# A list scheduler's figures and its model of transfers, replaced in a two-layer decoder kernel

## The chip, the cores and the metric

The kernel runs on one core of one Trainium2 chip. The metric is the device time of one execution in microseconds (us), lower is better. Traces come from the hardware profiler; in them PE is TensorE (matmuls), PEld its weight loads, DVE is VectorE, ACT is ScalarE, POOL is GpSimd and SP is SyncE, whose queue issues most DMAs.

## The reference

Two layers, post-norm. Layer 0 mixes tokens by a chunked causal gMLP, layer 1 by causal attention in one block of 256 keys (12 heads of 64); beside each runs a 4-head cross-attention into 256 memory tokens. Sequence 256, width 1024, feed-forward width 2816, float32 throughout.

```python
for i in range(2):
    if i == 0:
        u, v, q_mem = split(x @ a_w_in)          # 768, 768, 256
        mix = gmlp_mixer(u, v, ...)              # gelu, layer norm of v, W_s v + b, times u
    else:
        q, k, v, q_mem = split(x @ b_w_in)       # 768, 768, 768, 256
        mix = causal_attention(q, k, v)          # 12 heads
    mem_out = memory_cross_attention(q_mem, mem, w_mem_kv[i])
    sub = concatenate([mix, mem_out]) @ w_mix_out[i]
    x = layer_norm(ALPHA * x + sub)
    g, u = split(x @ w_ffn_in[i])                # 2 x 2816
    x = layer_norm(ALPHA * x + (silu(g) * u) @ w_ffn_out[i])
return x
```

## The kernel before

**Work.** Every weight is read once, as float32, in units of mostly 1 MiB (128 x 2048) that SP's queue loads from one flat array in the order in which they are used. A unit lands in a raw buffer (a ring of four, `raw`; two of the four quarter matrices of an S unit, below, go to buffers of their own, tags `gb` and `vbig`). Each half of it is then split in two: ACT copies it to a rounded `hi` (a CAST in the trace), DVE subtracts to get `lo` (a TENSOR_TENSOR into the same tile, `spl_...`). PE multiplies in three passes: hi by hi, hi by lo, lo by hi. Ten split halves can be held at a time (`HALF_BUFS`). The feed-forward goes by chunks of 256 columns: an R step takes one chunk directly (tiles `pf`, `pg`), an S unit takes two chunks together in seven products M1, M5, M2, M3, M6, M7, M4 (a Strassen form; tiles `X`, `Y`, `Z`, with letter f for layer 0 and g for layer 1). Three of the products need sums of quarter matrices, which DVE adds (`raw_s<-raw_s,raw_s`); the sum for M7 is made by a DMA from POOL's queue that adds into the raw buffer while it lands. After M6, ACT copies the sum from `X` to `u2`; M7 adds into `X` again, and so has to wait for that copy. Each layer has four S units. The kernel interleaves the products with the second matrix of the feed-forward (`fof`, `fog`).

**Order.** The code doesn't call the engines. It records operations (`Plan.add`, `Op`), and `Plan.emit` issues them in an order that `Plan.order` has worked out at build time by simulating the program with a duration for every operation. In every engine's queue the instructions run in that order, and one that waits holds up those behind it. PE's own order is that in which the code records its operations; the planner moves DVE, ACT, POOL and SP, and chooses buffer slots.

- `Op.cost` gives an operation `hold` (time before the engine takes the next) and `lat` (time until its result is there).
- `deadlines` puts PE's operations end to end and works back from them to a latest time `late` for every other operation, with `delay` as the distance of two dependent ones.
- `simulate` takes at each step the operation that can start first on any engine, the one with the smallest `late` among equals, and looks ahead: when one with an earlier `late` will become ready while the candidate runs, it takes a shorter one in between, or lets the engine idle. The three numbers of a setting (`slip`, `idle`, `margin`) rule that. `lost` sums the time that PE idles in the simulation.
- `order` runs the five settings of `TRIALS` and keeps the order with the least `lost`.
- A transfer in `simulate` before the change: one link of 437 bytes a ns for all queues, 2.3 us from issue to its first byte, 2.1 times the bytes and at least 7.8 us for a DMA of POOL.

Of the kernel before, what the change touches and what calls it, by code (L numbers as in the profile page):

```python
# [209 lines left out]
class Op:  # L210
# [13 lines left out]
    def cost(self):  # L224

        w = max([v.width() for v in self.writes + self.reads] or [1])
        e, n = self.engine, self.name
        if n == "dma_start":
            v = (self.writes or self.reads)[0]
            self.bytes = 4 * v.ap.ap[0][1] * v.width()  # L230
            self.hold, self.lat = (900 if e == "gpsimd" else 400), 0
        elif e == "tensor":
            w = self.args[2].width() if n == "matmul" else P
            f32 = n == "matmul" and self.args[2].root.dtype == F32
            self.hold = max(104, (w + 32) / 2.4) if not f32 else 0.85 * w
            self.lat = 200 + 0.37 * w if not f32 else self.hold + 270
        elif e == "vector":
            slow = n in ("tensor_scalar_mul", "tensor_scalar_add") or n == "tensor_copy"
            self.lat = 225 + 0.48 * w if n == "tensor_scalar_mul" and w > 8 else 150 + 1.042 * w
            self.hold = self.lat - 82  # L240
        elif e == "scalar":
            self.lat = 190 + 0.842 * w + (200 if "accum_out" in self.kw else 0)
            self.hold = self.lat - 100
        else:
            self.lat = self.hold = 700 + 2.5 * w if w < 8 else 250 + 2.0 * w


class Plan:
# [48 lines left out]
    def delay(self, a, b):  # L297

        if a.engine == b.engine and a.name != "dma_start":
            return a.hold  # L300
        if a.name == "dma_start":
            return 2300 + a.bytes / 400 if a.engine != "gpsimd" else 2300 + a.bytes / 180
        return a.lat + (50 if b.engine == "tensor" else 33)

    def deadlines(self):
        t = 4300
        for op in self.ops:
            if op.engine == "tensor":
                op.late = t
                t += op.hold  # L310
        for op in self.ops:
            for o in op.before.values():
                o.after.append(op)
        slots, last, follow = {}, {}, {}
        for op in self.ops:
            for b in op.roots:
                last[b] = op.n
        for op in self.ops:
            for b in op.roots:
                if b.tile is None and b.slot is None:  # L320
                    free = slots.setdefault(b.tag, [(0, i, None) for i in range(b.bufs)])
                    free.sort()
                    n, b.slot, was = free.pop(0)
                    if was:
# [12 lines left out]

    def order(self):
        self.deadlines()
        best = None  # L340
        for trial in self.TRIALS:
            for op in self.ops:
                for b in op.roots:
                    b.slot, b.last, b.left = None, 0.0, 0
            for op in self.ops:
                for b in op.roots:
                    b.left += 1
            out, lost = self.simulate(*trial)
            self.trials.append(lost)
            if best is None or lost < best[0]:  # L350
                best = lost, [(op, op.opens, op.call, op.start, op.end, [b.slot for b in op.opens]) for op in out]
        for op, op.opens, op.call, op.start, op.end, slots in best[1]:
            for b, b.slot in zip(op.opens, slots):
                pass
        return [x[0] for x in best[1]]

    def simulate(self, slip, idle, margin):
# [2 lines left out]
        head = {e: 0 for e in by_late}  # L360
        gone = set()
        free = {e: 0.0 for e in self.ENGINES}
        busy = dict(free)
        waiting = {op.n: len(op.before) for op in self.ops}
        at = {op.n: 0.0 for op in self.ops}
# [2 lines left out]
        for op in self.ops:  # L368
            for b in op.roots:
                if b.tile is None:  # L370
                    t = tags.setdefault(b.tag, {"queue": [], "slots": [(0.0, i) for i in range(b.bufs)]})
                    if b not in t["queue"]:
                        t["queue"].append(b)
        pe = [op for op in self.ops if op.engine == "tensor"]
        ip = 0
        link = 0.0
        for op in self.ops:
            if not waiting[op.n]:
                for e in op.calls():
                    ready[e].append(op)  # L380
        out = []

        def opening(op):

            t0 = at[op.n]
            for b in op.roots:
                if b.slot is not None or b.tile is not None:
                    continue
# [5 lines left out]
                fit = [x for x in t["slots"] if not b.whole or x[1] in whole]  # L394
                if not fit:
                    return None
                t0 = max(t0, min(fit)[0])
            return t0

        def hope(op, memo, depth):  # L400

            if op in memo:
                return memo[op]
            t = at[op.n]
            if waiting[op.n]:
                for o in op.before.values():
                    if o in gone:
# [12 lines left out]
        while len(out) < len(self.ops):  # L420
# [64 lines left out]
            for b in op.opens:  # L485
                q = tags[b.tag]
                q["queue"].remove(b)
                fit = [x for x in q["slots"] if x[0] <= t] if not b.whole else [x for x in q["slots"] if x[1] in whole]
                s = min([x for x in fit if x[1] not in whole] or fit) if b.psum else min(q["slots"])
                q["slots"].remove(s)  # L490
                b.slot = s[1]
            if e == "tensor" and (op.name == "transpose" or op.kw["start"]):
# [2 lines left out]
                if b.tag == "mm":  # L495
                    (whole.add if full else whole.discard)(b.slot)
            if op.name == "dma_start":
                size = op.bytes * (2.1 if e == "gpsimd" else 1) / 437
                link = max(link, t + 2300) + size
                end = max(link, t + 7800 if e == "gpsimd" else 0) + 100  # L500
            else:
                end = t + op.call.lat
            op.end = end
            out.append(op)
            for o in op.after:
                w = t + op.call.hold if o.engine == e and not o.other and op.name != "dma_start" else end + (50 if o.engine == "tensor" else 33)
                at[o.n] = max(at[o.n], w)
                waiting[o.n] -= 1
                if not waiting[o.n] and o.engine != "tensor":
                    for e2 in o.calls():  # L510
                        ready[e2].append(o)
            for b in op.roots:
                b.left -= 1
                b.last = max(b.last, end + 33)
                if not b.left and b.slot is not None:
                    tags[b.tag]["slots"].append((b.last, b.slot))
        return out, lost

    def emit(self):
# [934 lines left out]
```

## Time and profile before

| | us |
|---|---|
| median of 3 runs (lowest, highest) | 569.29 (568.52, 570.24) |
| the profiled execution's own time | 569.77 |
| its span, first to last instruction | 568.1 |
| around the span | 1.67 |
| mean granted TensorE clock in the span | 0.997 |

Rows of the trace below come from the profiled execution; "own time" means its 569.77 us. All recorded operations carry one source line, L527, that of the call in `emit`, so groups are told apart by the names of the tiles.

### The profile page before, as it was taken

Reading aid. Unit: us, or ns where it says so; the run is one execution under the profiler, and the core shown is the slowest. Engines: PE = TensorE matmul, PEld = TensorE weight load, DVE = VectorE, ACT = ScalarE, POOL = GpSimd, SP = SyncE. Lnnn points to the kernel's source line nnn. Section 1 sums busy time; section 2 is a strip of 40 time slices with the busy share of each in tenths; the row PEclk is TensorE's granted clock in tenths of the full one; section 3 lists DMA queues with packets and bytes.
Section 4 is the critical chain, followed back from the end, with each engine's and each line's share of the span. In section 5 each row is a group of like instructions: output and inputs, shape, how many; then the busy total and the mean of one; then the engine's idle time right before and its main releaser. Section 6 shows DMA issues by size and latency. Waiting matters only on the chain.

```text
span 568.1 us, 8078 instructions
## 1 busy us (share of the span) xinstructions
PE 554.7 (98%) x3052; PEld 478.0 (84%) x3052; DVE 498.8 (88%) x667; ACT 363.6 (64%) x550; POOL 23.0 (4%) x32
## 2 busy tenths in 40 slices
PE   8999999999999999999999999999999999999994
PEld 7999879887888778888899999888788888878884
DVE  5689889999999999994887889589998999989965
ACT  6676757677676757763446988654766676757710
POOL 2101001000000000000000000000000000000001
PEclk9999999999999999999999999999999999999998
DMA  8999744736856685775367343346448757675502
GB/s 292 359 388 345 308 170 137 291 74 247 228 195 228 195 313 150 295 279 193 118 230 300 141 149 106 118 148 240 149 133 303 213 211 216 212 281 133 207 1 75
DMA packets 21624, 118.89 MB, mean 209 GB/s; under 512 B 2384, under 2 KB 6096, under 8 KB 9168
## 3 DMA queue, kind: packets, MB, share of 16 engines
q1 hardware_dynamic: 20000, 109.45, 52.4%
q0 software_dynamic: 1152, 8.39, 8.0%
q10 hardware_dynamic: 432, 0.52, 0.3%
q8 instruction: 24, 0.39, 0.3%
q14 instruction: 16, 0.13, 0.1%
HBM read 117.31 MB, written 1.05 MB: 208 GB/s over the span
## 4 chain that ended last, share of the span: by engine, by line
PE 47%; DVE 25%; issue 5%; DMA 4%; ACT 3%; DVEq 0%; ACTq 0%
PE fog L527 7%; PE fof L527 7%; DVE spl_s_M L527 6%; PE Xg L527 5%; PE Xf L527 4%; DMA raw_s<-in_w 4%; DVE raw_s L527 4%; PE opc L527 4%; PE bv L527 3%; PE qk L527 3%; PE pg L527 2%; PE Zf L527 2%; PE pf L527 2%; PE Zg L527 2%; DVE spl_w L527 1%
## 5 line engine op out<-in xcount | busy, mean ns | idle before, releaser
L527 ACT CAST spl_s_M<-raw_s 128x1024 fp32r<-128x1024 f32 x112 | 115.4, 1052 | 56.2 <-DVE raw_s L527 20.3
L527 DVE TENSOR_TENSOR spl_s_M<-raw_s,spl_s_M 128x1024 fp32r<-128x1024 f32 x112 | 132.2, 1219 | 5.8 <-ACT spl_s_M L527 5.4
L527 PE MATMUL fog<-spl_w,htg 128*128 128x512 f32 (+1 forms) x282 | 63.7, 378 | 0.0
L527 PE MATMUL fof<-spl_w,htf 128*128 128x512 f32 x264 | 63.7, 392 | 0.0
L527 PEld LDWEIGHTS fog<-spl_w,htg 128*128 128x128 f32 x282 | 50.2, 188 | 9.4
L527 PEld LDWEIGHTS fof<-spl_w,htf 128*128 128x128 f32 x264 | 49.0, 188 | 9.9
L527 DVE TENSOR_TENSOR spl_w<-raw_w,spl_w 128x1024 fp32r<-128x1024 f32 x44 | 53.2, 1218 | 2.3 <-ACT spl_w L527 2.3
L527 DVE TENSOR_TENSOR raw_s<-raw_s,raw_s 128x2048 f32<-128x2048 f32 x24 | 54.9, 2286 | 0.1
L527 ACT CAST spl_w<-raw_w 128x1024 fp32r<-128x1024 f32 x44 | 45.8, 1050 | 13.7 <-PE fog L527 3.8
L527 PE MATMUL qk<-x2T,spl_qk 128*128 128x256 f32 x288 | 36.5, 284 | 0.1
L527 PEld LDWEIGHTS qk<-x2T,spl_qk 128*128 128x128 f32 x288 | 35.2, 192 | 0.4 <-DVE mix L527 0.3
L527 PE MATMUL Xf<-spl_s_M,SfM 128*128 128x512 f32 x96 | 23.2, 390 | 0.6 <-ACT u2f L527 0.6
L527 PE MATMUL Xg<-spl_s_M,SgM 128*128 128x512 f32 x96 | 23.2, 390 | 0.3 <-ACT u2g L527 0.3
L527 PE MATMUL opc<-spl_o,mix 128*128 128x512 f32 x96 | 23.1, 394 | 0.0
L527 PE MATMUL Zf<-spl_s_M,SfM 128*128 128x512 f32 x96 | 23.1, 389 | 0.0
L527 PE MATMUL Zg<-spl_s_M,SgM 128*128 128x512 f32 x96 | 23.1, 389 | 0.0
L527 PE MATMUL Xg<-spl_s_M,x3T 128*128 128x512 f32 x96 | 22.8, 391 | 0.0
L527 PE MATMUL Xf<-spl_s_M,x1T 128*128 128x512 f32 x96 | 22.7, 391 | 0.0
L527 PE MATMUL opa<-spl_o,mix 128*128 128x512 f32 x96 | 22.5, 392 | 0.0
L527 PEld LDWEIGHTS Xf<-spl_s_M,SfM 128*128 128x128 f32 x96 | 17.9, 188 | 4.7 <-ACT u2f L527 1.0
L527 PEld LDWEIGHTS Xg<-spl_s_M,SgM 128*128 128x128 f32 x96 | 17.9, 188 | 4.4 <-ACT u2g L527 0.7
L527 PEld LDWEIGHTS Xg<-spl_s_M,x3T 128*128 128x128 f32 x96 | 17.9, 188 | 4.2 <-DVE m5g L527 0.4
(232 smaller groups left out, 1082.9 us busy)
## 6 DMA issues: line engine op xcount, KB each, us to landing
raw_s<-in_w SPq DMA_DIRECT2D x32, 1024.0 KB, 5.9
raw_w<-in_w SPq DMA_DIRECT2D x22, 1024.0 KB, 5.5
raw_o<-in_w SPq DMA_DIRECT2D x8, 1024.0 KB, 6.4
raw_s<-in_w POOLq DMA_DIRECT2D x8, 1024.0 KB, 8.8
raw_r_A<-in_w SPq DMA_DIRECT2D x6, 1024.0 KB, 4.9
raw_r_B<-in_w SPq DMA_DIRECT2D x6, 1024.0 KB, 4.8
raw_qk<-in_w SPq DMA_DIRECT2D x6, 1024.0 KB, 5.8
raw_u<-in_w SPq DMA_DIRECT2D x3, 1024.0 KB, 9.8
```

What stands on the lines that cost most here:

```text
L527: getattr(getattr(self.nc, c.engine), c.name)(*map(real, c.args), **{k: real(v) for k, v in c.kw.items()})
```

## The change

The figures in `Op.cost` and `delay` are replaced, and the model of transfers becomes a class of its own, `Wire`. It keeps two queues, one for SP and ACT (`hard`) and one for POOL (`soft`), each moving one transfer at a time, at 250, 370 or 428 bytes a ns by the time since the start for the one, 223 for the other, and 155 and 123 when both move. A transfer starts 2.35 us after its issue. It has an `end`, and a later `sure`: 0.2 us after its last byte in the first 20 us, then 1.2 us after it (1.8 us for POOL). Operations that need the data, and buffers that it wrote, count from `sure`. SP may issue its next DMA only when the one eight places before has ended. An operation on DVE or ACT that depends on one of the same engine counts from that one's result plus 35 ns, where it counted from its `hold`; a consumer on POOL counts 500 ns after the result. SP starts at 0.8 us. Nothing else of the kernel is edited: the recorded operations, PE's order and `TRIALS` are the same.

```diff
@@ Op.cost
+        psum = any(v.root.psum for v in self.writes + self.reads)
...
-            self.hold, self.lat = (900 if e == "gpsimd" else 400), 0
+            self.hold, self.lat = (1000 if e == "gpsimd" else 450), 0
...
-            self.lat = 200 + 0.37 * w if not f32 else self.hold + 270
+            self.lat = (205 + 0.36 * w if n == "matmul" else 273) if not f32 else self.hold + 280
         elif e == "vector":
-            slow = n in ("tensor_scalar_mul", "tensor_scalar_add") or n == "tensor_copy"
-            self.lat = 225 + 0.48 * w if n == "tensor_scalar_mul" and w > 8 else 150 + 1.042 * w
+            fast = n == "tensor_scalar_mul" and w > 8
+            self.lat = 225 + 0.48 * w if fast else 152 + 1.042 * w
+            if n == "scalar_tensor_tensor" and not psum:
+                self.lat += 57
             self.hold = self.lat - 82
         elif e == "scalar":
-            self.lat = 190 + 0.842 * w + (200 if "accum_out" in self.kw else 0)
-            self.hold = self.lat - 100
+            self.lat = 190 + 0.842 * w + (90 if "accum_out" in self.kw else 0) - (35 if psum else 0)
+            self.hold = self.lat - 98 + (100 if "accum_out" in self.kw else 0)
         else:
-            self.lat = self.hold = 700 + 2.5 * w if w < 8 else 250 + 2.0 * w
+            self.lat = self.hold = 985 if w < 8 else 300 + 1.4 * w
+
+class Wire:
+
+    HARD, SOFT, BOTH, LANES = ((7000, 250), (30000, 370), (1e12, 428)), 223, (155, 123), 8
+    SPARE = 1200, 1800
+
+    def __init__(self):
+        self.now, self.hard, self.soft, self.sent = 0.0, [], [], []
+
+    def lane(self):
+        return self.sent[-self.LANES].end + 30 if len(self.sent) >= self.LANES else 0.0
+
+    def issue(self, op, t):
+        self.run(t, [self.hard, self.soft])
+        if op.engine == "sync":
+            self.sent.append(op)
+        (self.soft if op.engine == "gpsimd" else self.hard).append([op, t + 2350, op.bytes])
+        self.run(1e12, [[list(x) for x in q] for q in (self.hard, self.soft)])
+
+    def run(self, until, queues):
+        hard, soft = queues
+        now = self.now
+        while (hard or soft) and now < until:
+            live = [bool(q) and q[0][1] <= now for q in queues]
+            edge, hard_rate = next(x for x in self.HARD if now < x[0])
+            rates = self.BOTH if all(live) else (hard_rate * live[0], self.SOFT * live[1])
+            ends = [now + q[0][2] / r for q, r, a in zip(queues, rates, live) if a]
+            stop = min(ends + [edge] + [q[0][1] for q, a in zip(queues, live) if q and not a] + [until])
+            for q, r, a in zip(queues, rates, live):
+                if a:
+                    q[0][2] -= (stop - now) * r
+                    if q[0][2] < 1:
+                        op = q.pop(0)[0]
+                        op.end = stop + 100
+                        op.sure = stop + (self.SPARE[op.engine == "gpsimd"] if stop > 20000 else 200)
+            now = stop
+        if until < 1e12:
+            self.now = until

@@ Plan.delay
-            return a.hold
+            return a.hold if a.engine == "tensor" else a.lat + 35
...
-        return a.lat + (50 if b.engine == "tensor" else 33)
+        return a.lat + {"tensor": 56, "gpsimd": 500}.get(b.engine, 35)

@@ Plan.simulate
+        free["sync"] = 800.0
...
+        def free_at(x):
+            b = x[0]
+            return max([b.last] + [o.sure for o in b.moves]) if b else 0.0
+
         def opening(op):
-            t0 = at[op.n]
+            t0 = max([at[op.n]] + [o.sure for o in op.moves])
+            if op.engine == "sync":
+                t0 = max(t0, wire.lane())
...
-                t0 = max(t0, min(fit)[0])
+                t0 = max(t0, min(map(free_at, fit)))
...
         def hope(op, memo, depth):
-            t = at[op.n]
+            t = max([at[op.n]] + [o.sure for o in op.moves if o in gone])
...
             if op.name == "dma_start":
-                size = op.bytes * (2.1 if e == "gpsimd" else 1) / 437
-                link = max(link, t + 2300) + size
-                end = max(link, t + 7800 if e == "gpsimd" else 0) + 100
+                wire.issue(op, t)
+                end = 0
...
             for o in op.after:
-                w = t + op.call.hold if o.engine == e and not o.other and op.name != "dma_start" else end + (50 if o.engine == "tensor" else 33)
-                at[o.n] = max(at[o.n], w)
+                if op.name != "dma_start":
+                    same = o.engine == e == "tensor"
+                    at[o.n] = max(at[o.n], t + op.call.hold if same else end + {"tensor": 56, "gpsimd": 500}.get(o.engine, 35))
```

## Rows read from the trace of the kernel before

**Rows 1.** Part 1 of the profile's page: busy us of each engine, its share of the span, number of instructions.

```profile
PE 554.7 (98%) x3052; PEld 478.0 (84%) x3052; DVE 498.8 (88%) x667; ACT 363.6 (64%) x550; POOL 23.0 (4%) x32
```

**Rows 2.** The table of stretches: from and to in us, length, then busy us of each engine (and instructions), granted clock, DMA's busy share, GB/s.

```profile
0.00:14.20 14.20, 12.21 (x74) 10.74 (x75) 7.63 (x15) 8.71 (x16) 3.63 (x12) 1.00 0.86 292
14.20:28.40 14.20, 14.20 (x97) 14.20 (x96) 8.52 (x13) 8.81 (x13) 1.64 (x1) 1.00 1.05 359
...
190.00:205.00 15.00, 14.63 (x68) 12.26 (x69) 15.00 (x14) 10.28 (x12) 0.00 (x0) 1.00 0.65 238
...
550.00:568.10 18.10, 10.65 (x64) 9.33 (x62) 11.01 (x25) 0.51 (x1) 2.20 (x3) 0.91 0.18 60
```

**Rows 3.** PE's waits in the whole span: who waited for whom, us in total, times, longest.

```profile
PE sm L527 <- DVE klm L527: 0.6, 1, 0.6
PE Xf L527 <- ACT u2f L527: 0.6, 1, 0.6
PE pu L527 <- DVE spl_u L527: 0.5, 1, 0.5
...
PE tpf L527 <- DVE hf L527: 0.4, 1, 0.4
PE tpf L527 <- DVE m5f L527: 0.4, 1, 0.4
...
PE pf L527 <- DVE x1T L527: 0.3, 1, 0.3
PE Xg L527 <- ACT u2g L527: 0.3, 1, 0.3
PE tpg L527 <- DVE hg L527: 0.2, 1, 0.2
```

**Rows 4.** ACT's waits for landings of weights, same columns.

```profile
ACT spl_s_M L527 <- DMA raw_s<-in_w: 13.6, 5, 4.1
...
ACT spl_o L527 <- DMA raw_o<-in_w: 5.2, 3, 4.3
...
ACT spl_u L527 <- DMA raw_u<-in_w: 4.7, 3, 3.3
```

**Rows 5.** Timelines of ACT and PE around the scores of the memory attention, in layer 0 and (last two rows) layer 1: start us, us, engine, operation, how many in a run, and in brackets the idle time before it and who ended it.

```profile
56.19 1.05 ACT L527 CAST spl_o<-raw_o 128x1024 fp32r<-128x1024 f32 x1 [4.29 <-DMA raw_o<-in_w]
57.15 1.13 ACT L527 CAST kkm<-hkm 64x256 fp32r<-64x256 f32 x3
...
47.16 5.92 PE L527 MATMUL hkm<-memT,spl_km 128*128 128x256 f32 x48
...
58.77 0.28 PE L527 MATMUL sm<-kkm,qqm 128*128 128x256 f32 x1
...
62.80 1.47 PE L527 MATMUL pvm<-spl_vm,memT 128*128 128x256 f32 x11
...
337.37 0.39 PE L527 MATMUL sm<-kkm,qqm 128*128 128x256 f32 x1
...
338.31 0.28 PE L527 MATMUL sm<-klm,qqm 128*128 128x256 f32 x1
```

**Rows 6.** DMA issues: how many, KB of one, median us from issue to landing.

```profile
raw_s<-in_w SPq DMA_DIRECT2D x32, 1024.0 KB, 5.9
...
raw_r_B<-in_w SPq DMA_DIRECT2D x6, 1024.0 KB, 4.8
...
raw_u<-in_w SPq DMA_DIRECT2D x3, 1024.0 KB, 9.8
```

**Rows 7.** Around M6 and M7 of an S unit in layer 0: SP's timeline, one row of the chain that ended last (start us, us, what), ACT's and PE's timelines; the last three rows are the same place in layer 1.

```profile
198.82 0.33 SPq L527 DMA_DIRECT2D raw_w<-in_w  x1
...
201.03 6.39 DMA raw_s<-in_w
...
207.52 2.00 ACT L527 CAST spl_s_M<-raw_s 128x1024 fp32r<-128x1024 f32 x2 [4.09 <-DMA raw_s<-in_w]
...
210.37 0.57 ACT L527 COPY u2f<-Xf 128x512 f32<-128x512 f32 x1
...
204.83 2.88 PE L527 MATMUL Xf<-spl_s_M,SfM 128*128 128x512 f32 x12
207.55 2.88 PE L527 MATMUL fof<-spl_w,htf 128*128 128x512 f32 x12
211.00 3.02 PE L527 MATMUL Xf<-spl_s_M,SfM 128*128 128x512 f32 x12 [0.56 <-ACT u2f L527]
...
502.70 2.00 ACT L527 CAST spl_s_M<-raw_s 128x1024 fp32r<-128x1024 f32 x2 [3.79 <-DMA raw_s<-in_w]
...
503.05 2.88 PE L527 MATMUL fog<-spl_w,htg 128*128 128x512 f32 x12
506.18 3.02 PE L527 MATMUL Xg<-spl_s_M,SgM 128*128 128x512 f32 x12 [0.26 <-ACT u2g L527]
```

**Rows 8.** Timeline of DVE, two pairs of neighbours: in the first the second works on the first one's result, in the other the two are independent.

```profile
550.92 0.69 DVE L527 SCALAR_TENSOR_TENSOR xres<-xres,fog 128x512 f32<-128x512 f32 x1 [0.45 <-PE fog L527]
551.64 0.69 DVE L527 BATCH_NORM_STATS2 stg<-xres 128x6 f32<-128x512 f32 x1
...
178.22 0.68 DVE L527 TENSOR_TENSOR m1f<-m1f,Yf 128x512 f32<-128x512 f32 x1
178.82 0.68 DVE L527 TENSOR_TENSOR u2f<-u2f,Zf 128x512 f32<-128x512 f32 x1
```

More of the change, by code (lines that the diff above doesn't have):

```diff
@@ L311, in deadlines @@
         for op in self.ops:
+            op.moves = [o for o in op.before.values() if o.name == "dma_start"]
             for o in op.before.values():
@@ L343, in order @@
                 for b in op.roots:
-                    b.slot, b.last, b.left = None, 0.0, 0
+                    b.slot, b.last, b.left, b.moves = None, 0.0, 0, []
             for op in self.ops:
@@ L370, in simulate @@
                 if b.tile is None:
-                    t = tags.setdefault(b.tag, {"queue": [], "slots": [(0.0, i) for i in range(b.bufs)]})
+                    t = tags.setdefault(b.tag, {"queue": [], "slots": [(None, i) for i in range(b.bufs)]})
                     if b not in t["queue"]:
@@ L375, in simulate @@
         ip = 0
-        link = 0.0
+        wire = Wire()
         for op in self.ops:
@@ L487, in simulate @@
                 q["queue"].remove(b)
-                fit = [x for x in q["slots"] if x[0] <= t] if not b.whole else [x for x in q["slots"] if x[1] in whole]
-                s = min([x for x in fit if x[1] not in whole] or fit) if b.psum else min(q["slots"])
+                fit = [(free_at(x), x[1], x) for x in q["slots"] if not b.whole or x[1] in whole]
+                if b.psum:
+                    fit = [x for x in fit if x[0] <= t and x[1] not in whole] or fit
+                s = min(fit, key=lambda x: x[:2])[2]
                 q["slots"].remove(s)
@@ L497, in simulate @@
             if op.name == "dma_start":
-                size = op.bytes * (2.1 if e == "gpsimd" else 1) / 437
-                link = max(link, t + 2300) + size
-                end = max(link, t + 7800 if e == "gpsimd" else 0) + 100
-            else:
-                end = t + op.call.lat
-            op.end = end
+                wire.issue(op, t)
+                end = 0
+            else:
+                op.end = end = t + op.call.lat
             out.append(op)
             for o in op.after:
-                w = t + op.call.hold if o.engine == e and not o.other and op.name != "dma_start" else end + (50 if o.engine == "tensor" else 33)
-                at[o.n] = max(at[o.n], w)
+                if op.name != "dma_start":
+                    same = o.engine == e == "tensor"
+                    at[o.n] = max(at[o.n], t + op.call.hold if same else end + {"tensor": 56, "gpsimd": 500}.get(o.engine, 35))
                 waiting[o.n] -= 1
@@ L513, in simulate @@
                 b.left -= 1
-                b.last = max(b.last, end + 33)
+                b.last = max(b.last, end + 35)
+                if op.name == "dma_start":
+                    b.moves.append(op)
                 if not b.left and b.slot is not None:
-                    tags[b.tag]["slots"].append((b.last, b.slot))
+                    tags[b.tag]["slots"].append((b, b.slot))
         return out, lost
```

## The prediction, made before the changed kernel was run

> **What bounds the kernel now.** I began with the busy times of the whole span: PE works for 554.7 us of 568.1, so it idles 13.4 us, and all the others idle more [rows 1]. The reader is to see that PE sets the time, and, since the change leaves PE's instructions and their order alone, that it can move nothing but these 13.4 us. Next the table of stretches: 7.45 us of them (18.10 - 10.65) lie after 550 us, in the closing chain of statistics, scale and stores behind the last matmuls, where order is forced by dependence; 1.99 us (14.20 - 12.21) lie in the first 14.2 us, where DMA is busy 0.86 of the time and the first weights land [rows 2]. That leaves 3.9 us in the middle. The clock is 1.00 in both early stretches and in the stretch at 190 us, the 2.4 GHz level, so none of it is a slower clock.
>
> The waits of PE by releaser show where these sit: eight of them behind the first 14 us, 0.2 to 0.6 us each, 3.3 us together [rows 3]. A matmul's shown end is modelled: a run of twelve with 512 columns is shown as 2.88 us while the next begins 2.72 us after it [rows 7], so each wait is really 0.16 us longer than it is shown, and what the middle can give back is 3.9 + 11 x 0.16 = 5.7 us at most (the eight waits and, as an estimate, three shorter ones between the score matmuls).
>
> Then I asked who was late. ACT waits 23.5 us in 11 waits for landings of weights, up to 4.3 us in one [rows 4]. ACT idles 36% of the span, so that costs nothing by itself; what costs is the work queued behind the waiting cast. Two places show it.
>
> First, at 56 us: ACT waits 4.29 us for `raw_o`, and the casts `kkm<-hkm` run only behind it, from 57.15. Their input was complete at 53.08 (47.16 + 5.92). PE comes to the scores at 58.77 and needs 4.03 us (to 62.80) for sixteen `sm` matmuls; in layer 1 eight of them start within 0.94 us, 0.134 each, so sixteen should take 2.15. Lost: 1.9 us [rows 5].
>
> Second, in the S units: at 207.52 ACT has waited 4.09 us for the first quarter of the next unit, casts it (2.00 us) and one `spl_w`, and only then copies `u2f` at 210.37. PE had issued the last matmul of its input by 207.55, and the product after it, M7, starts at 211.00 instead of 207.55 + 2.72 = 210.27: 0.73 us lost. In layer 1 the same: a wait of 3.79 us until 502.70, and M7 at 506.18 instead of 503.05 + 2.72 = 505.77: 0.41 us lost [rows 7].
>
> **The change part by part.**
>
> *Transfers.* The planner of before put a lone 1 MiB load at 2.3 + 1,048,576 / 437 = 2.40, + 0.1 = 4.8 us. The median landing of `raw_r_B` is 4.8 us: right when the queue is empty. `raw_s` takes 5.9 us in the median [rows 6]. Worked for the case at 201.03: the load before it went out at 198.82, so the old link gives 198.82 + 2.3 + 2.40 + 2.40 + 0.1 = 206.02; the chain has it landing 6.39 us after issue, at 207.42, 1.4 us later than planned [rows 7]. The new model gives 198.82 + 2.35 + 2.45 + 2.45 + 1.2 = 207.27. It also puts the copy of `u2f` at about 207.6, so at most one cast of a microsecond comes before it (two are shown as 2.00 us); then the copy of 0.57 us ends near 208.8, 1.4 us ahead of M7. I count the two stalls of 0.73 and 0.41 as gone but for wakeups: -1.1 us. The bounds are 0 (another cast takes the place) and -1.1.
>
> The Trainium skill's page "DMA: Bandwidth & Descriptors", section "Anatomy of one DMA", fits one DMA as about 2.0 us plus bytes over 436 GB/s, hence 4.4 us for 1 MiB: by that the old figures were right and the sum for this part would be 0. The trace disagrees wherever a load follows another (6.39 us).
>
> *The same at 56 us.* With 1.2 us of margin, and the slower rates before 30 us, `raw_o` is expected after the 53.08 at which `kkm` can start, so the casts go first. From 57.15 on they and their subtractions took until PE was served; 4 us earlier they are ready at 58.77. -1.9 us is the bound; I take -1.7, since the first score matmuls keep short waits. The other bound is 0: the cast of `raw_o` stays ahead.
>
> *The first loads.* PE waits 0.5 us at `pu` for `spl_u` [rows 3], and ACT 4.7 us for `raw_u` [rows 4], whose landing took 9.8 us in the median [rows 6]. SP's eight-place limit is now in the plan, so `raw_u` may move ahead of loads that are needed later. But DMA is busy 1.05 of the time in this stretch [rows 2]; bytes must be moved anyway. -0.3 us, bounds -0.7 and +1.5 (half a megabyte in front of a needed load at 359 GB/s).
>
> *Dependent operations on one engine.* A DVE result used by the next DVE operation: start to start 0.72 us (550.92 to 551.64), where two independent ones go 0.60 us apart (178.22 to 178.82) [rows 8]. The new `lat` + 35 ns is what the row shows; the old plan was 0.12 us short at each such link. Four of PE's waits, twice `tpf`, `pf` and `tpg`, 1.3 us as shown [rows 3], are for results of DVE, and no landing stands in their rows. Here the order is drawn anew, with somewhat better figures. I take 0; the bounds are -1.9 (all four go: 1.3 + 4 x 0.16) and +1.9 (as many come).
>
> *The rest.* POOL's and SP's new holds, the accumulate figures and the 500 ns to POOL cost nothing, as POOL is busy 4% of the span [rows 1] and a figure that is too high only lets its result be planned late; if that cover is gone, a sum for M7 is planned half a microsecond late. Where the stall of ACT goes: the fresh unit is cast after the copy, one cast later; that is also one subtraction later on DVE and one ring buffer freed later on SP's queue, behind which the next loads wait. In that stretch DVE is busy 15.00 of 15.00 us [rows 2], so this is not free if it repeats.
>
> *Sum:* -1.1 - 1.7 - 0.3 + 0 = -3.1 us on the own time of 569.77, that is 566.7. The own time lies 0.5 us over the median of the runs, so the median should be 566.2 us.
>
> **The rivals.**
>
> *All middle stalls go.* 5.7 us: 569.3 - 5.7 = 563.6. For it: the dependent links of DVE are now right too. Against: four of the eight waits have no landing in their rows, and DVE is full where they stand [rows 2].
>
> *Nothing measurable.* The two repairs happen, but the new order brings as many waits elsewhere as there are now on DVE (1.9 us) and some at the first loads (1.5 us); or the old figures were good enough, and only a margin is laid on top. 569.3, within 1.7. For it: PE's greatest single wait is 0.6 us as shown [rows 3], so three new ones of that size undo half of the gain. Against: the repair in the S units stands on a landing that the old figures miss by 1.4 us [rows 7]. Of its chance 0.05 is for the second half. The Trainium skill's fit in "DMA: Bandwidth & Descriptors" is the rule that speaks for that half.
>
> *Slower: the margin starves DVE in the S units.* For a lone load the new `sure` is 2.35 + 2.45 + 1.2 = 6.0 us while 4.8 is what such loads take [rows 6]. Its cast is then put behind other work of ACT for 1.2 us without need, and DVE, which is full, idles when it has nothing else ready. Eight S units x 1.2 = 9.6 us is the ceiling; if the ten split halves hide half of it, the time is 569.3 + 4.8 = 574. It decides from 0.2 us for each unit that reaches PE (8 x 0.2 = 1.6). Against: the plan fixes the order alone, so a cast that is next in its queue starts as soon as its data are there, and it is ACT that waits for these landings now [rows 4], not they for ACT.
>
> **How the numbers follow.** A change of 0.3% (1.7 us) is about what a measurement of this kernel can tell from none. Chances: the forecast 0.50 (its own range 564.5 to 567.6), all stalls gone 0.08, nothing measurable 0.25, slower 0.17. So faster 0.57, same 0.26, slower 0.17. The low end of the range is 569.3 - 5.7 with another 0.7 from the first loads, 562.9; the high end is 572.0: the unknown terms at their upper bounds with nothing won would be 569.3 + 1.9 + 1.5 = 572.7, and both at once are rare. About 0.1 is left out above it, of the slower case, and less below.
>
> **What would show it.** Right: ACT's waits for `raw_o` and `raw_s` fall well below 18.8 us; `kkm` is cast before the last `spl_o`; `u2f` and `u2g` are copied within 1.5 us of PE's end; PE's waits at `sm`, `Xf` and `Xg` are gone; PE's and DVE's busy times are as before. Wrong: the casts at these places are in the old order, or PE waits for `spl_s_M` or `spl_w`, of which [rows 3] has none; the last stretch is longer than 18.1 us; or DVE is idle in the stretch from 190 to 205 us, where it has no gap now [rows 2].

## The result, and the profile after

| | before | after |
|---|---|---|
| median of the runs taken side by side | 570.24 | 565.33 |
| lowest, highest | 568.52, 571.99 | 565.23, 567.35 |
| ratio after / before, 95% interval | | 0.9923 [0.9901, 0.9945] |
| the profiled execution's own time, its span | 569.77, 568.1 | 565.29, 563.6 |

The change makes the kernel 0.8% faster. The forecast was 566.2 us, its range 562.9 to 572.0, and "faster" had the largest chance. By the profiled executions the own time fell by 4.5 us, where the sum had 3.1. Part 1 of the page of after answers to [rows 1]:

```profile
PE 550.9 (98%) x3052; PEld 478.1 (85%) x3052; DVE 500.0 (89%) x667; ACT 362.9 (64%) x550; POOL 22.6 (4%) x32
```

The same instructions, and nearly the same busy times of all engines but PE. PE's shown busy time is 3.8 us lower (554.7 - 550.9), which is most of the 4.5: a part of a matmul's wait is shown as busy time, as in M7's 3.02 us behind its stall [rows 7], where after has 2.88 without one. So the places below are compared by the starts of matmuls and not by idle time. The table of stretches (columns as in [rows 2]):

```profile
14.20:28.40 14.20, 14.20 (x97) 14.20 (x96) 11.29 (x17) 11.91 (x19) 0.00 (x0) 1.00 1.03 402
190.00:205.00 15.00, 15.00 (x68) 12.43 (x67) 15.00 (x14) 10.67 (x12) 0.00 (x0) 1.00 0.77 284
550.00:563.60 13.60, 6.16 (x36) 5.27 (x34) 7.11 (x17) 0.51 (x1) 1.72 (x3) 0.92 0.23 78
```

PE fills the stretch at 190 us, DVE still has no gap there, and after 550 us PE idles 13.60 - 6.16 = 7.44 us, where it idled 7.45. PE's waits of after, but for the warm-up's, answer to [rows 3]:

```profile
PE qk L580 <- DVE mix L580: 1.4, 1, 1.4
PE va L580 <- ACT spl_v L580: 1.3, 1, 1.3
...
PE pt L580 <- DVE mix L580: 0.7, 1, 0.7
PE tpf L580 <- DVE hf L580: 0.6, 1, 0.6
```

`sm`, `Xf`, `Xg`, `pu` and `pf` are gone, and two larger ones for `mix` in layer 1 are new. Because PE's 3052 matmuls stand in the same order in every kernel here, each can be laid beside itself, and the shift of its start against before can be summed by place. The table is worked out that way from the traces, in us, negative where time came back; places below 0.15 are left empty, and the last column is the median of the runs.

| kernel | first loads (to the end of `pu`'s wait) | `sm`, layer 0 | S units (`Xf`, `Xg`) | `tpf`, `pf`, `tpg`, `pg` | attention (`qk`, `pt`, `s`) | other | all | median |
|---|---|---|---|---|---|---|---|---|
| after | -0.85 | -2.12 | -2.05 | -1.34 | +1.84 | | -4.49 | 565.33 |
| 1 `kkm` first | -0.65 | -2.12 | -0.86 | -0.60 | | +1.05 | -3.20 | 568.63 |
| 2 `u2` first | -0.41 | | +0.71 | | | | +0.33 | 570.14 |
| 3 transfers alone | | -2.12 | -2.09 | -1.35 | | | -5.71 | 563.72 |
| 4 costs and links alone | +1.14 | +0.84 | +1.21 | -0.49 | +1.49 | | +4.15 | 573.01 |
| 5 ACT's figures back | -0.95 | -2.12 | -2.09 | -0.98 | -0.19 | | -6.18 | 563.49 |
| 6 no margin | -0.67 | -0.99 | -2.09 | -1.14 | +1.82 | | -3.06 | 566.80 |
| 7 margin alone | -0.68 | +1.10 | -2.11 | -0.63 | | +0.91 | -1.50 | 567.52 |
| 8 no eight places | +1.99 | -0.87 | -2.09 | -1.36 | +1.86 | | -0.46 | 568.88 |
| 9 reads' figures back | -0.48 | -2.12 | -2.09 | -1.32 | +1.59 | | -4.41 | 565.19 |
| 10 PSUM figure back | +0.26 | -2.12 | -2.09 | -1.00 | +0.89 | | -4.09 | 564.87 |
| 11 before, other setting | -0.96 | +0.46 | -1.25 | +1.29 | | | -0.45 | 570.32 |
| 12 transfers, other setting | -1.34 | -2.12 | -2.11 | -0.92 | | | -6.50 | 563.29 |

One trace stands for each row, and the first loads differ by up to 1.2 us between kernels that issue them in the same order (runs 5 and 10), so a median can stand a microsecond from what its row says. Run 1 shows how far this goes: its profiled execution, 566.59 us, was the fastest of ten with a median of 568.63, and its row has -0.65, -0.60 and -0.86 at places whose order is that of before. A single value of a column is therefore weak; what many rows agree on is not.

**Where it came from.** ACT's and PE's timelines of after around the memory attention's scores (compare [rows 5]):

```profile
52.27 0.74 ACT L580 CAST kkm<-hkm 64x256 fp32r<-64x256 f32 x2 [1.43 <-PE hkm L580]
...
56.62 2.00 ACT L580 CAST spl_o<-raw_o 128x1024 fp32r<-128x1024 f32 x2
...
57.91 0.28 PE L580 MATMUL sm<-kkm,qqm 128*128 128x256 f32 x1
...
59.83 3.04 PE L580 MATMUL pvm<-spl_vm,memT 128*128 128x256 f32 x24
```

`kkm` is cast as soon as PE has made it, the last two casts of `spl_o` come behind it, and sixteen `sm` matmuls take 59.83 - 57.91 = 1.92 us, where they took 4.03. The S unit of [rows 7], ACT and PE:

```profile
199.95 1.05 ACT L580 CAST spl_w<-raw_w 128x1024 fp32r<-128x1024 f32 x1 [0.30 <-PE Zf L580]
202.74 1.05 ACT L580 CAST spl_s_M<-raw_s 128x1024 fp32r<-128x1024 f32 x1 [1.74 <-DMA raw_s<-in_w]
203.97 0.59 ACT L580 COPY u2f<-Xf 128x512 f32<-128x512 f32 x1 [0.18 <-PE Xf L580]
204.46 1.05 ACT L580 CAST spl_s_M<-raw_s 128x1024 fp32r<-128x1024 f32 x1
...
201.05 2.88 PE L580 MATMUL Xf<-spl_s_M,SfM 128*128 128x512 f32 x12
203.77 2.88 PE L580 MATMUL fof<-spl_w,htf 128*128 128x512 f32 x12
206.49 2.88 PE L580 MATMUL Xf<-spl_s_M,SfM 128*128 128x512 f32 x12
```

Two casts have moved. `spl_w`, which waits for no late landing, now goes ahead of the quarter that lands late, and the copy of `u2f` stands between that quarter's two halves. M7 starts 2.72 us after the product before it: no stall. But here the load also came sooner: its first cast starts 5.49 us after the issue (197.25 to 202.74), where it took 6.49 (201.03 to 207.52). In the old order M7 started 3.48 us after that cast (207.52 to 211.00). By that it would be due at 206.22 here, in time for 206.49, so this trace doesn't show that the order was needed at this place. It does so in layer 1, ACT and PE:

```profile
500.43 1.05 ACT L580 CAST spl_s_M<-raw_s 128x1024 fp32r<-128x1024 f32 x1 [2.43 <-DMA raw_s<-in_w]
...
499.42 2.89 PE L580 MATMUL fog<-spl_w,htg 128*128 128x512 f32 x12
502.14 2.91 PE L580 MATMUL Xg<-spl_s_M,SgM 128*128 128x512 f32 x12
```

The cast comes 1.01 us behind the start of `fog`. By the old order M7 would start 3.48 us after it, at 503.91; with one half and a `spl_w` less ahead of the copy it starts at 502.14, without a stall. ACT still waits for landings, for `raw_s` longer than before (compare [rows 4]):

```profile
ACT spl_s_M L580 <- DMA raw_s<-in_w: 18.8, 10, 3.2
```

**What was given back.** DVE, ACT and PE of after in layer 1:

```profile
331.71 0.17 DVE L580 RECIPROCAL zb<-zb 128x2 f32<-128x2 f32 x1 [0.35 <-ACT pb L580]
...
333.52 1.22 DVE L580 TENSOR_TENSOR spl_o<-raw_o,spl_o 128x1024 fp32r<-128x1024 f32 x1 [0.19 <-ACT spl_o L580]
334.66 0.75 DVE L580 TENSOR_TENSOR mix<-pv,mix 128x256 fp32r<-128x256 f32 x2
...
332.46 1.03 ACT L580 CAST spl_o<-raw_o 128x1024 fp32r<-128x1024 f32 x1
333.39 0.36 ACT L580 CAST mix<-pv 128x256 fp32r<-128x256 f32 x1
...
335.13 2.05 PE L580 MATMUL qk<-x2T,spl_qk 128*128 128x256 f32 x15 [1.36 <-DVE mix L580]
```

On both engines a half of `spl_o`, which PE needs later, stands ahead of the `mix` that PE needs next; DVE stood idle 0.35 us earlier, waiting for the sums `pb`. This is the +1.84 of the table, with 0.7 at `pt`.

### The profile page after: what moved, and what is told of

It reads as the page before. It is cut to its first block, busy times and chain, and to the rows that moved or that the text cites. A ratio compares the mean times of both kernels' runs of the same rounds, so it can differ in the third digit from the quotient of the medians.

```text
span 563.6 us, 8072 instructions
## 1 busy us (share of the span) xinstructions
PE 550.9 (98%) x3052; PEld 478.1 (85%) x3052; DVE 500.0 (89%) x667; ACT 362.9 (64%) x550; POOL 22.6 (4%) x32
## 3 DMA queue, kind: packets, MB, share of 16 engines
HBM read 117.31 MB, written 1.05 MB: 210 GB/s over the span
## 4 chain that ended last, share of the span: by engine, by line
PE 86%; ACT 6%; DVE 5%; issue 1%; DMA 1%; SPq 0%; DVEq 0%; ACTq 0%
PE fog L580 11%; PE fof L580 11%; PE Xg L580 8%; PE Xf L580 8%; PE pg L580 6%; PE pf L580 5%; PE opa L580 4%; PE Zg L580 4%; PE Zf L580 4%; PE opc L580 3%; PE pu L580 3%; PE bv L580 3%; PE va L580 2%; PE hkm L580 2%; PE hqm L580 2%; PE Yf L580 2%
## 5 line engine op out<-in xcount | busy, mean ns | idle before, releaser
L580 ACT CAST spl_s_M<-raw_s 128x1024 fp32r<-128x1024 f32 x112 | 115.1, 1052 | 56.4 <-DMA raw_s<-in_w 18.8
L580 PEld LDWEIGHTS Zg<-spl_s_M,SgM 128*128 128x128 f32 x96 | 18.0, 188 | 3.7
```

Source lines behind the costliest of these rows:

```text
L580: getattr(getattr(self.nc, c.engine), c.name)(*map(real, c.args), **{k: real(v) for k, v in c.kw.items()})
```

## The experiments

First the two repairs of the forecast by hand, in the old order (`held_back` moves one operation, with those that depend on it, behind another).

**1. `kkm` first.**

```diff
+        ops = self.held_back(ops, act("spl_o0_3_0")[0], klm)   # klm: the first four subtractions
```

> The kernel before, with one edit of its finished order: the cast of the first half of the last layer-0 output weight, which waited 4.29 us for its landing, and its subtraction on DVE, go behind the casts and subtractions of the memory keys. The planner's figures are untouched. Theory 'landings' (a cast that waits for a landing planned too early holds up what is queued behind it, and that is where the change gains): PE's steps at the score matmuls (sm) shrink by 1.9 to 2.1 us, all else stays, time 0.3 to 0.4% lower (567.9 to 568.3 beside 570.2). Rival 'redraw' (the stalls of before are an accident of that order and not of this wait): the sm steps stay within 0.5 us or the saving is lost before the next stage ends.

Measured: 568.63 us, ratio 0.9991 [0.9973, 1.0010]: by the runs nothing measurable, where 567.9 to 568.3 was expected. The 2.12 us at `sm` came back, as priced; but DVE and PE show what the old stall had covered:

```profile
72.36 2.35 DVE L554 TENSOR_TENSOR spl_km<-raw_km,spl_km 128x1024 fp32r<-128x1024 f32 x2
74.63 1.28 DVE L554 COPY pTm<-ptm 128x512 f32<-128x512 f32 x2
...
75.36 1.95 PE L554 MATMUL pvm<-pTm,svm 128*64 128x256 f32 x16 [0.98 <-DVE pTm L554]
```

PE, 2 us earlier, runs into two subtractions that stand ahead of a copy it needs. The cause of the `sm` stall is shown; undone alone, half of it is only moved.

**2. `u2` first.**

```diff
+        for name, u2 in (("spl_w0_5_1", "u2f6"), ("spl_s0_8_M1_1", "u2f6"), ("spl_w1_6_1", "u2g7"), ("spl_s1_9_M1_1", "u2g7")):
+            if ops.index(act(name)[0]) < ops.index(act(u2)[0]):
+                ops = self.held_back(ops, act(name)[0], act(u2)[:1])
```

> The kernel before, with its finished order edited in the last S unit but one of each layer: the copy of u2 goes ahead of the second cast of the next unit's first quarter and of one cast of an output weight. Figures untouched. 'Landings': the two stalls at M7 (0.73 and 0.41 us) and the smaller ones at M4 just behind (0.2 each) go, together 1.1 to 2.0 us; time 0.2 to 0.35% lower. 'Redraw', or DVE as the true limit in these units: M7 starts in time, but PE stops elsewhere within the same unit or the next, and the sum over the unit changes by less than 0.5 us.

Measured: 570.14 us, ratio 1.0007 [0.9996, 1.0018]. M7 gained 0.86 and 0.55 us at the two places, and PE's waits show new ones in the same kind of place:

```profile
PE Xf L555 <- DVE m5f L555: 0.6, 1, 0.6
...
PE Xf L555 <- ACT u2f L555: 0.5, 1, 0.5
PE Xg L555 <- DVE m5g L555: 0.5, 1, 0.5
```

In five of the eight S units of before the copy of `u2` stands behind two casts of the next quarter and one of `spl_w`; two were mended by name, another one stalled at its M7, and behind them M4 waited for DVE. A cause that sits in the planner's figures is not removed by moving one instruction.

**3. The transfers alone** (class `Wire`, its margin and the eight places; costs and links as before).

```diff
-                link = max(link, t + 2300) + size
-                end = max(link, t + 7800 if e == "gpsimd" else 0) + 100
+                wire.issue(op, t)
```

> The kernel before with the new transfer model alone: the class Wire with its rates, its eight places and its margin, SP from 0.8 us; durations of operations and the distance of dependent ones as before. 'Landings': the gains at sm, M7, M4 and at the first u projection (5.0 us together between the two traces) are all here, those at DVE's results (tpf, tpg, pf, pt, 1.6 us) are not, and of the 2.1 us newly lost in layer 1's attention part or all is gone, as it is drawn anew: 565.0 to 567.5. 'Redraw': some other sum, anywhere within 2 us of before, with stalls left at sm or M7.

Measured: 563.72 us, ratio 0.9897 [0.9883, 0.9912]: by the medians more than the whole change, though the two intervals overlap. PE's waits behind the start:

```profile
PE pf L577 <- DVE x1T L577: 0.3, 1, 0.3
PE pt L577 <- DVE mix L577: 0.2, 1, 0.2
PE pg L577 <- DVE htg L577: 0.2, 1, 0.2
```

**4. All but the transfers** (`Op.cost`, `delay` and the distance between dependent operations).

```diff
-                w = t + op.call.hold if o.engine == e and not o.other and op.name != "dma_start" else end + (50 if o.engine == "tensor" else 33)
+                w = t + op.call.hold if o.engine == e == "tensor" else end + {"tensor": 56, "gpsimd": 500}.get(o.engine, 35)
```

> The kernel before with all of the change but its transfer model: new durations in cost, results of the same engine counted from lat + 35 ns, 500 ns to POOL; one link of 437 bytes a ns as before. 'Landings': ACT's long waits and PE's stalls at sm, Xf, Xg stay (4 us), only stalls at DVE's results may go (up to 1.6 us): 568.5 to 571. 'Redraw', or better durations as the source of the gain: 565 to 567.5, with sm and M7 served in time.

Measured: 573.01 us, ratio 1.0063 [1.0041, 1.0086]: slower than before. The stalls at `sm` and in the S units are there, and new ones:

```profile
PE tpf L530 <- DVE hf L530: 1.0, 1, 1.0
PE sm L530 <- DVE klm L530: 0.9, 2, 0.5
PE Xf L530 <- ACT u2f L530: 0.8, 1, 0.8
```

Together with run 3: the transfer model makes the whole gain, and the other figures by themselves make the kernel 0.6% slower.

**5. ACT's figures back** (the whole change, ACT's `hold` and `lat` as before).

```diff
-            self.lat = 190 + 0.842 * w + (90 if "accum_out" in self.kw else 0) - (35 if psum else 0)
-            self.hold = self.lat - 98 + (100 if "accum_out" in self.kw else 0)
+            self.lat = 190 + 0.842 * w + (200 if "accum_out" in self.kw else 0)
+            self.hold = self.lat - 100
```

> The whole change, but the two lines with ACT's hold and lat as they were (accumulating activations: a result 200 ns after the plain one, where the change says 90). In the trace of the changed kernel an exponential of 128 columns started at 331.19 and its sum was read until 331.68, 0.49 us; the old figure is 0.50, the new one 0.39. Theory 'accumulate' (this figure is what brings PE's new waits for mix in layer 1, 1.4 and 0.7 us, since the softmax is planned to end 0.1 us early and a weight's cast goes ahead of mix): both waits go, the rest stays; 563.0 to 564.3 beside 565.3. Rival 'links' (the dependence of one engine's operations, or the redraw by all figures, brings them): both waits stay or others of the same size come; 565 to 566.

Measured: 563.49 us, ratio 0.9872 [0.9830, 0.9913]; the attention's +1.84 is -0.19. DVE at the same place:

```profile
331.41 1.22 DVE L580 TENSOR_TENSOR spl_o<-raw_o,spl_o 128x1024 fp32r<-128x1024 f32 x1
332.55 0.16 DVE L580 RECIPROCAL zb<-zb 128x2 f32<-128x2 f32 x1
```

The subtraction of `spl_o` now fills DVE's wait for `pb`, and no half of a weight stands ahead of `mix`. So ACT's new figures cost 1.8 us. The medians say it (565.33 - 563.49, though from two sets whose intervals overlap), and so does the column: the kernels in which one or both of these figures are new (after, runs 4, 6, 8, 9 and 10) have +0.89 to +1.86 there, the others at most 0.2 either way. That is all that separates the whole change from the transfers alone; the DVE costs and links are worth next to nothing beside the new transfers: with them 563.49, without them (run 3) 563.72.

**6. No margin** and **7. the margin alone** (in the model of before).

```diff
-    SPARE = 1200, 1800
+    SPARE = 200, 200
```

```diff
-                end = max(link, t + 7800 if e == "gpsimd" else 0) + 100
+                end = max(link, t + 7800 if e == "gpsimd" else 0) + (100 if link < 20000 else 1800 if e == "gpsimd" else 1200)
```

> The whole change, but data count as usable 0.2 us after their last byte all along (the margin of 1.2 and 1.8 us is taken away). Theory 'rates' (the rates and the queue bring the gain, the margin is spare): as the changed kernel, 565.0 to 566.0, no stall at sm, Xf or Xg. Theory 'margin' (the hand edit at the memory keys and the landings 1.2 us after the modelled last byte say that it is needed): ACT waits for the output weight ahead of the memory keys' casts again, PE loses up to 2 us at sm, and M7 stalls of 0.3 to 0.8 us come back in some S units; 566 to 569.

> The kernel before, with its link of 437 bytes a ns, its durations and its links, and the margin alone: landings 1.2 us (1.8 for POOL) later, once the link has passed 20 us. 'Rates': a constant doesn't mend the first 57 us, where DMA is the limit and the plan is some 4 us early, so sm (2.1 us) and pu (0.8 us) stay; M7's stalls may halve: 568.5 to 570. 'Margin': M7's and sm's stalls go: 566 to 567.5.

Measured: 566.80, ratio 0.9947 [0.9922, 0.9972], and 567.52, ratio 0.9944 [0.9922, 0.9967]. The S units are mended in both, by the table to the same 2.1 us; `sm` in neither. ACT of run 6, then of run 7:

```profile
54.74 1.05 ACT L580 CAST spl_o<-raw_o 128x1024 fp32r<-128x1024 f32 x1 [4.21 <-PE sv L580]
55.69 1.90 ACT L580 CAST kkm<-hkm 64x256 fp32r<-64x256 f32 x5
```

```profile
56.35 1.05 ACT L527 CAST spl_o<-raw_o 128x1024 fp32r<-128x1024 f32 x1 [4.26 <-DMA raw_o<-in_w]
57.31 1.13 ACT L527 CAST kkm<-hkm 64x256 fp32r<-64x256 f32 x3
```

Both have the old order at `sm`: the cast of `raw_o`, waiting over 4 us, ahead of `kkm`. In run 6 the row names PE (`sv`) for the end of the wait: the load had landed at 54.28, 0.46 us before the cast, so there the landing was not the last thing that it waited for. The margin is worth about 1.5 us of the whole change by the medians (566.80 - 565.33, with intervals that overlap), 1.1 of it at `sm` by the table.

**8. Without SP's eight places.**

```diff
-                t0 = max(t0, wire.lane())
+                pass
```

> The whole change, but SP may issue at any time in the plan (the wait for the DMA eight places before is taken out of the model; it stays in the program). Theory 'places' (this rule alone moves the loads of the u weights ahead of the gate's tables, as SP's order of the changed kernel has them, and gives back the 0.8 us at pu): the loads return to the old order, pu's stall of 0.5 to 0.8 us returns; all else as the changed kernel: 565.8 to 566.8. Rival 'early rates' (250 and 370 bytes a ns order the first loads): no change, 565.0 to 565.7.

Measured: 568.88, ratio 0.9977 [0.9955, 1.0000]. SP of run 8 and then of after, and PE of run 8:

```profile
11.98 2.17 SPq L580 DMA_DIRECT2D mraw<-in_memT  x4
14.69 0.34 SPq L580 DMA_DIRECT2D raw_qm<-in_w  x1
...
25.22 1.70 PE L580 MATMUL hqm<-x0T,spl_qm 128*128 128x256 f32 x12 [0.75 <-DVE spl_qm L580]
27.70 2.53 PE L580 MATMUL hqm<-x0T,spl_qm 128*128 128x256 f32 x19 [0.79 <-DVE spl_qm L580]
```

```profile
10.32 0.33 SPq L580 DMA_DIRECT2D raw_qm<-in_w  x1
...
12.58 0.34 SPq L580 DMA_DIRECT2D raw_u<-in_w  x1
...
18.19 0.87 SPq L580 DMA_DIRECT2D wsT<-in_wsT  x1
```

Without the limit the plan lets four loads of `mraw` go ahead of `raw_qm`, which is issued 4.4 us later, and PE waits at `hqm`: 2.8 us lost at the first loads, and `sm` keeps its old order as well. The stall at `pu`, which I had expected back, is not there. Runs 6 and 8 show that `sm` is mended only with both the margin and the places in the model; whether the rates are needed too was not tried, as run 7 lacks rates and places together.

**9 and 10. Which of ACT's figures?**

```diff
-            self.lat = 190 + 0.842 * w + (90 if "accum_out" in self.kw else 0) - (35 if psum else 0)
-            self.hold = self.lat - 98 + (100 if "accum_out" in self.kw else 0)
+            self.lat = 190 + 0.842 * w + (200 if "accum_out" in self.kw else 0) - (35 if psum else 0)
+            self.hold = self.lat - 98
```

```diff
-            self.lat = 190 + 0.842 * w + (90 if "accum_out" in self.kw else 0) - (35 if psum else 0)
+            self.lat = 190 + 0.842 * w + (90 if "accum_out" in self.kw else 0)
```

> The whole change, with the figures for a sum read behind an ACT operation as before (200 ns more for the result, nothing more for the next operation), but the 35 ns off for ACT's work on PSUM kept. If the reads' figures made the two waits for mix in layer 1 (1.21 and 0.78 us), both are gone and the median is 563.5 us. If the 35 ns made them, both stay and it is 565.3 us. In this order a mix subtraction stands on DVE behind two klq ones at the first place, and the order at the second place is that of the whole change: I expect the second wait to stay and the first to shrink, about 564.5 us.

> The whole change without the 35 ns off for ACT's work on PSUM, the reads' new figures kept. If the 35 ns put the mix casts behind others, the second wait (0.78 us at pt) is gone and the first (1.21 us at qk) shrinks to a few tenths: about 563.8 us. If the reads' figures did it, both waits stay and the median is 565.3 us.

Measured: 565.19, ratio 0.9926 [0.9898, 0.9953], and 564.87, ratio 0.9922 [0.9897, 0.9947]. By the start of the one matmul that waits, against before, after has +1.23 at `qk` and +0.89 at `pt`. With the reads' old figure both places went the other way from what I expected: `pt` fell to +0.37 and `qk` rose to +1.48. With the PSUM figure back both shrank, to +0.81 and +0.24, but less than expected, and the median stayed near 565; in its trace the first loads lie 1.1 us behind those of after. Either half alone leaves about 565 us; it took both back (run 5) to reach 563.5. That the pair costs 1.8 us is shown, that one figure of it does is not.

**11. Another setting of before**, and **12. the transfers alone under that setting.**

```diff
-    TRIALS = ((150, 1500, 800), (150, 1000, 500), (300, 1500, 1200), (100, 700, 300), (300, 2500, 1600))
+    TRIALS = ((100, 700, 300),)
```

> The kernel before with one other look-ahead setting (100, 700, 300) and every figure and the transfer model as before: 12 of ACT's operations, 31 of DVE's and 3 of SP's change place. If any fresh order removes the late waits, because they are an accident of one order, it gains 2 us or more, like the margin alone (567.5 us or less). If they come from the figures, sm's 2.1 us and the 0.4 to 0.8 us at the S units stay and the rest moves by less than 1.2 us either way: 568 to 571 us. The second is what I expect.

> The transfer model alone, as in the third experiment, under the look-ahead setting of the eleventh (100, 700, 300): 29 of ACT's operations, 37 of DVE's and 1 of SP's change place against the third, and in the S units the copy of u2 stands behind two casts of the next unit again. If the gain is the transfer model's and not that of one lucky order, sm's 2.1 us and the first loads' 0.7 us stay won, the S units' 0.8 to 1.2 us may be lost, and the median is 564 to 566 us. If the third experiment was one lucky draw, it is back at 568 us or more. I expect 565 us.

Measured: 570.32, ratio 1.0010 [0.9991, 1.0028], and 563.29, ratio 0.9874 [0.9844, 0.9904]. A fresh order under the old figures moved stalls about (S units -1.25, DVE's results +1.29) and left `sm`; under the transfer model it kept all of the gain. So that does not hang on one draw. I was wrong on one point in run 12: `u2f` stands behind two casts there, and nothing stalls.

```profile
199.26 1.06 ACT L577 CAST spl_w<-raw_w 128x1024 fp32r<-128x1024 f32 x1 [0.30 <-PE Zf L577]
201.14 2.00 ACT L577 CAST spl_s_M<-raw_s 128x1024 fp32r<-128x1024 f32 x2 [0.82 <-DMA raw_s<-in_w]
203.28 0.59 ACT L577 COPY u2f<-Xf 128x512 f32<-128x512 f32 x1
```

The ready `spl_w` goes first, and the load was issued at 195.55, 7.5 us ahead of PE's `fof` at 203.08. In before it is 6.5 us (201.03 and 207.55), in after 6.5 as well (197.25 and 203.77), with the sooner landing shown above. In run 11, where ACT's order at this place is that of before, it is 7.7 us (199.01 and 206.71), and nothing stalls either. Run 1 has the order of before there too and issues 6.7 us ahead (198.52 and 205.19); its cast starts 5.97 us after the issue (204.49), and M7 comes 2.78 us after `fof`, hardly late. The stall hung on about a microsecond, and a new order (layer 1 of after), an earlier issue or a sooner landing can give it.

Runs 3, 5 and 12 have the lowest medians, about 2 us below the change, and none of their executions (562.94 to 564.28) reaches the change's lowest (565.23). They were taken in other sets, and the intervals of their ratios overlap the change's and one another's, so that they beat it is likely, and which of them is best stays open.

## Why the prediction was right, and where its steps were off

- **What bounds it.** Right that PE sets the time and that the last stretch stays: it idles 7.44 us. Wrong that only idle time can move: PE's went from 13.4 to 12.7 us (563.6 - 550.9), and 3.8 us came out of what is shown as busy. The count of eight waits behind the first 14 us also leaves out a ninth, `pt` for `mix`, 0.2 us.
- **Transfers, -1.1.** Right in mechanism, too small: the S units gave 2.05. At M7 0.86 and 0.52 came back, and 0.33 and 0.35 at M4, the next product into `X`, which I had not listed: I read two stalls and missed what each left behind. How much of it is the order's is less sure: the old order stalled M7 of layer 0 by 0.73 us in before's trace and by 0.06 in run 1's. And "the copy first" was half of the reason; the other is that the ready `spl_w` moved ahead (runs 7 and 12).
- **`sm`, -1.7.** 2.12; no short waits stayed, and the sixteen matmuls take 1.92 us, 0.12 each, where I had put 0.134 by layer 1. Run 1 shows the cause, and also that the sum was safe only because the rest of the order was drawn anew: by hand the same repair loses 1.05 us at 75 us, and by its median nothing measurable is won.
- **First loads, -0.3.** The column has 0.85; `pu`'s wait, 0.77, is gone in a kernel where `raw_u` goes ahead of `wsT`, and the rest differs from one execution to the next: run 1, with the loads of before and `pu`'s wait still there, has 0.65. So the size of this gain is not shown. The eight places that I named are worth more, 2.8 us (run 8), because the rest of the model would have drawn a worse order without them.
- **Dependent links, 0 within 1.9.** -1.34 at the four places, near the bound; but other orders under the old links gained there too (run 3: -1.35; run 1, with before's order there, -0.60), so the links are not needed for it.
- **"The rest" at nothing.** This is the step that failed. I covered the accumulate figures with POOL's idle time and with "a figure that is too high only lets its result be planned late". ACT's new figures are lower, and lateness in planning is what reorders: they cost 1.8 us (run 5), +1.84 in the table. That they stood in the same sentence as POOL's hid them. Which of the two figures does it stays open (runs 9 and 10). The error was offset by the four terms above, which together came out 3.3 us larger than I had put them, so that the total lies 0.9 us from the median is in part luck.
- **The rivals.** "All middle stalls go", 563.6 us at a chance of 0.08, is the time that the kernels with the new transfers and ACT's old figures reach (563.72, 563.49, 563.29), though a few middle waits stay in each; ACT's new figures are why it didn't happen. "The margin starves DVE" did not: 15.00 of 15.00 us at 190 us, and without the margin the kernel is no faster (run 6). "Nothing measurable" is out by the interval.
- **The signs.** `kkm`, `u2f`, PE's waits and DVE's busy time read right. Three did not hold: PE's busy time fell by 3.8 us; one `u2g` is copied 1.80 us after PE's end (499.58 to 501.38) and not within 1.5, without a stall; and ACT's waits for landings did not fall below 18.8 us, they are 18.8 for `raw_s` alone. A wait of an idle engine is no measure; what stands behind it is.

The rule of the Trainium skill that spoke against the change ("DMA: Bandwidth & Descriptors", "Anatomy of one DMA") gives 4.4 us for 1 MiB as an estimate; its fit is for DMAs that GpSimd issues, and these loads are SP's. After, by the page of the profile:

```profile
raw_s<-in_w SPq DMA_DIRECT2D x32, 1024.0 KB, 6.1
```

`raw_r_B`, whose loads go out 3 us or more after the one ahead of them, takes 4.8 us in both kernels ([rows 6], and the same page of after), near that rule; a load close behind another isn't, and the margin laid on the old figures (run 7) already gains 0.56%.

## What to carry to other kernels

A list scheduler's order is as good as its figure for when data arrive: correct that first, with the queue's limits and a margin, since an in-order engine that waits for a late landing holds up ready work behind it. Figures of single operations that change by 0.1 us or less can still draw a worse order, so put each group of figures on the chip alone. A stall read in one execution may be absent from another of the same order, so look at a second trace before you price it. Where a hand repair at one place gives nothing, look for the next stall that the first one covered.

## What the runs showed of the hardware that was not expected

- In the stretch from 14.2 to 28.4 us of after, the transfers moved 402 GB/s, where before moved 359 [rows 2] with the DMA engines as busy (1.03 and 1.05) and other loads among them; what made the difference was not tried. The Trainium skill ("DMA: Bandwidth & Descriptors", "Where 436 GB/s comes from") says that about 358 GB/s, one core's limit on the HBM side, binds for loads from HBM, and in the same place that its own 16 MB measurement of 425 GB/s is near the fabric's rate. This trace, of a kernel on one core, disagrees with the first: 402.
- ACT's sum read shows as an instruction of its own behind each exponential of layer 1:

```profile
331.19 0.39 ACT L580 ACTIVATE pb<-pb,mb 128x128 f32<-128x128 f32 x1
331.49 0.19 ACT L580 ACTIVATION_READ_ACCUMULATOR pb<-pb,mb 128x1 f32 x1
```

The sum of 128 columns is there 0.49 us after the start (331.68 - 331.19). The old formula of `lat` gives 0.498 us for it, the new one 0.388: on this the figure before was nearer.
